# A Poisson loss on one Trainium2 core: one load instead of four ahead of the first barrier, the others after ScalarE's table load

## The chip, the core and the metric

The kernel runs on one core of a Trainium2 chip. The metric is the device time of an execution in microseconds, the median of several runs. A profile shows one execution as a *span*, from the first instruction counted to the last landing. Every ratio below is the mean time of one kernel's fast runs over that of the kernel before in the same rounds on the same chip, so it is not quite the ratio of the medians quoted beside it.

## The reference

```
log_input: [1024, 4096] float32      target: [1024, 4096] float32
loss = exp(log_input) - target * log_input
out  = mean(loss, axis=-1)           # 1024 values
```

The two inputs are 33.55 MB together and are read once. The result is 4 KB.

## The kernel before

Each of the 128 partitions holds eight rows of both inputs. ScalarE takes the exponential of `x` (the input `log_input`) with a running sum, VectorE multiplies `t` (`target`) by `x` with a running sum, and a small ScalarE activation joins the two sums of a row. SyncE issues all loads into one queue: four rows of `x`, four of `t`, two of each, one of each, and the last row in seven pieces (`TAIL`).

```
loads = []
for first, rows in ((0, 4), (4, 2), (6, 1)):
    loads += [("x", first * d, rows * d), ("t", first * d, rows * d)]
for what, w in TAIL:                         # the last row, in pieces
    loads.append((what, at[what], w * d // 128))
    ...
early = []
for i, (what, lo, w) in enumerate(loads):
    if what == "x" and lo in (6 * d, 7 * d): # buffers come free here
        nc.sync.wait_ge(exp_done, free)
        nc.sync.wait_ge(prod_done, free)
    dma = nc.sync.dma_start(out=place(what, lo, w), in_=src[:, lo : lo + w])
    dma.then_inc(landed[i] if i < len(loads) - 1 else last_ready, 16)
    if lo < 6 * d:
        early.append(dma.ins)                # x_big, t_big, x_mid, t_mid
before_first_barrier(nc, early)              # moved ahead of SyncE's first drain
...
    nc.scalar.activation(out=e_dump[...], in_=place("x", lo, w), func=ACT_F.Exp,
                         accum_out=...).wait_op(landed[i], 16, "sem-ge")
```

A program begins with a barrier of all engines. `before_first_barrier` moves the given loads in front of it, so that data flow while the engines meet. Four loads go there: `x_big` and `t_big` (8.39 MB each), `x_mid` and `t_mid` (4.19 MB each). ScalarE's function table is loaded by an instruction of its own right before the first exponential, behind the barrier.

Of the kernel before, what the change touches and what calls it, by code (L numbers as in the profile page):

```python
# [5 lines left out]
ACT_F = mybir.ActivationFunctionType  # L6
ALU = mybir.AluOpType
F32 = mybir.dt.float32
# [5 lines left out]
def before_first_barrier(nc, instructions):  # L14





    here, first = nc.cur_bb.bb, nc.main_func.blocks[0]  # L20
    names = {i.name for i in instructions}
    here.instructions = [i for i in here.instructions if i.name not in names]
    at = next(
        k
        for k, i in enumerate(first.instructions)
        if i.engine == mybir.EngineType.SP and i.opcode == "Drain"
    )
    first.instructions = first.instructions[:at] + instructions + first.instructions[at:]


def kernel(tc, log_input, target, out):
# [14 lines left out]
    nc = tc.nc  # L46
# [3 lines left out]
    P = nc.NUM_PARTITIONS  # L50
    n, d = log_input.shape
# [41 lines left out]
    def place(what, lo, w):  # L93
        row = lo // d
        if 4 <= row < 6:
            return mid[what][:, lo - 4 * d : lo - 4 * d + w]
        if row >= 6:
            lo -= (6 if row == 6 else 4) * d
        return big[what][:, lo : lo + w]
# [4 lines left out]
    join_dump = nc.alloc_sbuf_tensor("join_dump", [P, 2 * last_row], F32).ap()  # L104
# [5 lines left out]
    landed = [nc.alloc_semaphore(f"landed{i}") for i in range(len(loads) - 1)]  # L110


    last_ready = nc.alloc_semaphore("last_ready")
    exp_done = nc.alloc_semaphore("exp_done")
    prod_done = nc.alloc_semaphore("prod_done")
    join_done = nc.alloc_semaphore("join_done")
    ones_done = nc.alloc_semaphore("ones_done")
    loss_done = nc.alloc_semaphore("loss_done")
    out_done = nc.alloc_semaphore("out_done")


    early = []
    for i, (what, lo, w) in enumerate(loads):
        if what == "x" and lo in (6 * d, 7 * d):
            free = 1 if lo == 6 * d else 4
            nc.sync.wait_ge(exp_done, free)
            nc.sync.wait_ge(prod_done, free)  # L127
        src = x_v if what == "x" else t_v
        dma = nc.sync.dma_start(out=place(what, lo, w), in_=src[:, lo : lo + w])  # L129
        dma.then_inc(landed[i] if i < len(loads) - 1 else last_ready, 16)  # L130
        if lo < 6 * d:
            early.append(dma.ins)
    before_first_barrier(nc, early)


    nc.gpsimd.memset(big["x"][:, 4 * d : 4 * d + n_parts], -1.0).then_inc(ones_done, 1)  # L136


    def join(row, exps):
        nc.scalar.wait_ge(exp_done, exps)  # L140
        nc.scalar.activation(  # L141
            out=join_dump[:, 2 * row : 2 * row + 2],
            in_=parts[:, 2 * row : 2 * row + 2],
            func=ACT_F.Copy,
            scale=inv_d,
            accum_out=all_loss[:, row : row + 1],
        ).wait_op(prod_done, row + 1, "sem-ge").then_inc(join_done, 1)

    for k, (lo, w, i) in enumerate(x_work):
# [3 lines left out]
        elif col == 0 and row == 1:  # L153
            nc.scalar.wait_ge(exp_done, k)
        nc.scalar.activation(  # L155
            out=e_dump[:, col : col + w],
            in_=place("x", lo, w),
            func=ACT_F.Exp,
            bias=0.0,
            scale=1.0,  # L160
# [8 lines left out]
    for j, (lo, w, i) in enumerate(t_work):  # L169
# [4 lines left out]
        if j < n_t - 1:  # L174
            nc.vector.tensor_tensor_reduce(  # L175
                out=place("t", lo, w),
                in0=place("t", lo, w),
                in1=place("x", lo, w),
                scale=-1.0,
# [9 lines left out]
        else:  # L189
# [4 lines left out]
                out=place("t", lo, w + n_parts),  # L194
                in0=place("t", lo, w + n_parts),
                in1=place("x", lo, w + n_parts),
                scale=-inv_d,
# [8 lines left out]
    nc.sync.dma_start(out=out_v, in_=all_loss).wait_op(loss_done, 1, "sem-ge").then_inc(  # L206
        out_done, 16
    )
    used = landed + [last_ready, exp_done, prod_done, join_done, ones_done, loss_done]
    nc.sync.sem_clear(range(used[0].num, out_done.num))  # L210
    assert all(used[0].num <= s.num < out_done.num for s in used)
    nc.sync.wait_ge(out_done, 16).then_inc(out_done, -16)
# [30 lines left out]
```

## Time and profile before

| | before |
|---|---|
| device time, median of the first 3 runs | 84.07 us (84.0 to 84.13) |
| span of the profiled run | 82.5 us |
| DMA queue's packets, share of 16 engines | 95.8% |
| VectorE, ScalarE busy | 43%, 40% |
| the four early issues | 0.00 to 1.87 us |
| table load | 2.93 to 4.21 us |
| first exponential, first product | 21.80 us, 41.12 us |

The question to ask of such a table is which row sets the end. The longest waits of the two compute engines answer it (engine, line, what it waited for, us in total, times, the longest one):

```profile
DVE t_big L175 <- DMA t_big<-in_target_dram: 43.4, 3, 41.1
ACT e_dump L155 <- DMA x_big<-in_log_input_dram: 23.6, 3, 17.6
```

Both compute engines stand still until data come. The prediction below reads the rest of the profile.

### The profile page before, as it was taken

The page shows a single profiled execution, that of the slowest core. Times are in us where ns is not written, and L with a number is a line of the kernel's source. Part 1 is how long each engine was busy: PE and PEld are TensorE (multiplying, and loading weights), DVE is VectorE, ACT ScalarE, POOL GpSimd, SP SyncE. Part 2 cuts the span into 40 slices and gives each one's busy share as a digit, 9 for nine tenths or more (in the row PEclk, how much of TensorE's full clock was granted, in tenths as well). Part 3 has the DMA queues.
Part 4 walks back from the last instruction along what each step waited for, and adds up shares of the span by engine and source line. Part 5 has one row for each costly group of instructions (what it writes and reads, how often), then busy time and mean ns, then how long its engine had stood idle before and what let it go on. Part 6 is the DMA issues. An engine that isn't in the chain of part 4 may idle for free.

```text
span 82.5 us, 131 instructions
## 1 busy us (share of the span) xinstructions
DVE 35.6 (43%) x22; ACT 33.2 (40%) x35; POOL 0.3 (0%) x5
## 2 busy tenths in 40 slices
DVE  0000000000000000000099999999369995993992
ACT  0500000000499920000000998979792496009460
POOL 0000000000000000000000000000000000000000
DMA  9289999929999992999599799799799999999960
GB/s 508 127 381 508 508 508 508 476 95 445 508 508 508 508 413 95 508 508 508 254 508 429 333 508 492 318 460 508 302 453 397 461 421 418 426 402 412 397 231 2
DMA packets 2016, 33.56 MB, mean 407 GB/s; under 512 B 352, under 2 KB 608, under 8 KB 1120
## 3 DMA queue, kind: packets, MB, share of 16 engines
q1 hardware_dynamic: 2016, 33.56, 95.8%
HBM read 33.55 MB, written 0.00 MB: 407 GB/s over the span
## 4 chain that ended last, share of the span: by engine, by line
DMA 72%; DVE 18%; issue 5%; SPq 3%; DVEq 0%
DMA t_big<-in_target_dram 49%; DMA x_big<-in_log_input_dram 23%; DVE t_big L175 17%; SPq L129 3%; DVE t_big L193 1%; DVE parts L175 0%; DVEq L192 0%; SPq L127 0%; DVE all_loss L193 0%
## 5 line engine op out<-in xcount | busy, mean ns | idle before, releaser
L175 DVE CUSTOM_DVE_ANT_0 t_big<-t_big,x_big 128x4096 f32<-128x4096 f32 (+3 forms) x8 | 26.2, 3308 | 43.5 <-DMA t_big<-in_target_dram 43.4
L155 ACT ACTIVATE e_dump<-x_big 128x4096 f32<-128x4096 f32 (+3 forms) x8 | 21.8, 2729 | 23.9 <-DMA x_big<-in_log_input_dram 23.6
L141 ACT ACTIVATE join_dump<-parts 128x2 f32<-128x2 f32 x7 | 1.4, 203 | 20.4 <-DVE parts L175 20.3
L175 DVE CUSTOM_DVE_ANT_0 t_mid<-t_mid,x_mid 128x4096 f32<-128x4096 f32 x2 | 8.8, 4424 | 2.0 <-DMA t_mid<-in_target_dram 2.0
L155 ACT ACTIVATE e_dump<-x_mid 128x4096 f32<-128x4096 f32 x2 | 7.1, 3568 | 0.0
L155 ACT ACT_TABLE_LOAD x1 | 1.3, 1283 | 2.9 <-PEq L48 2.9
L155 ACT ACTIVATION_READ_ACCUMULATOR e_dump<-x_big 128x1 f32 x8 | 1.5, 186 | 0.0
L141 ACT ACTIVATION_READ_ACCUMULATOR join_dump<-parts 128x1 f32 x7 | 1.3, 186 | 0.0
L175 DVE DVE_READ_ACCUMULATOR2_ANT parts<- 128x1 f32 x7 | 0.6, 84 | 0.0
L193 DVE CUSTOM_DVE_ANT_0 t_big<-t_big,x_big 128x390 f32<-128x390 f32 x1 | 0.6, 566 | 0.0
L155 ACT ACTIVATION_READ_ACCUMULATOR e_dump<-x_mid 128x1 f32 x2 | 0.4, 186 | 0.0
L175 DVE DVE_READ_ACCUMULATOR2_ANT t_big<- 128x1 f32 x3 | 0.2, 82 | 0.0
L136 POOL MEMSET x_big<- 128x6 f32 x1 | 0.1, 104 | 2.5 <-POOLq L48 2.5
L227 POOL MEMSET const-uint8-127<- 128x1 uint8 x1 | 0.1, 102 | 0.0
L227 POOL MEMSET const-bfloat16-1.0<- 128x1 bf16 x1 | 0.1, 101 | 0.0
L227 POOL MEMSET const-float32-0.0<- 128x1 f32 x1 | 0.1, 98 | 0.2 <-issue 0.2
L227 POOL MEMSET const-float32-1.0<- 128x1 f32 x1 | 0.1, 98 | 0.0
L193 DVE DVE_READ_ACCUMULATOR2_ANT all_loss<- 128x1 f32 x1 | 0.1, 82 | 0.0
## 6 DMA issues: line engine op xcount, KB each, us to landing
x_mid<-in_log_input_dram SPq DMA_DIRECT2D x1, 4096.0 KB, 49.9
t_mid<-in_target_dram SPq DMA_DIRECT2D x1, 4096.0 KB, 59.2
x_big<-in_log_input_dram SPq DMA_DIRECT2D x1, 2048.0 KB, 19.8
t_big<-in_target_dram SPq DMA_DIRECT2D x1, 2048.0 KB, 24.3
x_big<-in_log_input_dram SPq DMA_DIRECT2D x1, 1568.0 KB, 15.4
t_big<-in_target_dram SPq DMA_DIRECT2D x1, 800.0 KB, 17.0
t_big<-in_target_dram SPq DMA_DIRECT2D x1, 768.0 KB, 18.4
x_big<-in_log_input_dram SPq DMA_DIRECT2D x1, 384.0 KB, 18.9
```

The source lines that it names most:

```text
L129: dma = nc.sync.dma_start(out=place(what, lo, w), in_=src[:, lo : lo + w])
L136: nc.gpsimd.memset(big["x"][:, 4 * d : 4 * d + n_parts], -1.0).then_inc(ones_done, 1)
L141: nc.scalar.activation(out=join_dump[:, 2 * row : 2 * row + 2], in_=parts[:, 2 * row : 2 * row + 2], func=ACT_F.Copy, scale=inv_d, accum_o ...
L155: nc.scalar.activation(out=e_dump[:, col : col + w], in_=place("x", lo, w), func=ACT_F.Exp, bias=0.0, scale=1.0, accum_out=parts[:, 2 * ro ...
L175: nc.vector.tensor_tensor_reduce(out=place("t", lo, w), in0=place("t", lo, w), in1=place("x", lo, w), scale=-1.0, scalar=0.0, op0=ALU.mult ...
L193: nc.vector.tensor_tensor_reduce(out=place("t", lo, w + n_parts), in0=place("t", lo, w + n_parts), in1=place("x", lo, w + n_parts), scale= ...
L227: nc = _bacc.Bacc("TRN2", target_bir_lowering=False, num_devices=1)
```

## The change

Its intent is to let the engines through the first barrier sooner and to have ScalarE's table ready at once. Only the first load stays ahead of the barrier. A dummy exponential of a constant makes ScalarE load its table right after the barrier, and SyncE waits for it before it issues the second load.

```diff
+    table_done = nc.alloc_semaphore("table_done")
...
-    early = []
     for i, (what, lo, w) in enumerate(loads):
...
-        if lo < 6 * d:
-            early.append(dma.ins)
-    before_first_barrier(nc, early)
+        if i == 0:
+            before_first_barrier(nc, [dma.ins])
+            nc.sync.wait_ge(table_done, 1)
...
+    nc.scalar.activation(
+        out=join_dump[:, :1],
+        in_=nc.const_aps.tensor(0.0, [P, 1], F32),
+        func=ACT_F.Exp,
+        bias=0.0,
+        scale=1.0,
+    ).then_inc(table_done, 1)
```

The list of semaphores cleared at the end gets `table_done` too.

More of the change, by code (lines that the diff above doesn't have):

```diff
@@ L208 @@
     )
-    used = landed + [last_ready, exp_done, prod_done, join_done, ones_done, loss_done]
+    used = landed + [last_ready, exp_done, prod_done, join_done, ones_done, table_done, loss_done]
     nc.sync.sem_clear(range(used[0].num, out_done.num))
```

## The prediction

> **What bounds the kernel now.** I read the page first: the engine shares, the strip of 40 slices, and the chain that ended last.
>
> ```profile
> DVE 35.6 (43%) x22; ACT 33.2 (40%) x35; POOL 0.3 (0%) x5
> DMA  9289999929999992999599799799799999999960
> q1 hardware_dynamic: 2016, 33.56, 95.8%
> DMA 72%; DVE 18%; issue 5%; SPq 3%; DVEq 0%
> ```
>
> No compute engine is busy for half of the 82.5 us span, while the packets of the single queue fill 95.8% of the time of all 16 DMA engines. The few low digits in the DMA strip look like holes, so I asked for busy time in long stretches (columns after the window's length: DVE, ACT and POOL busy with instruction counts, PE clock, DMA share, GB/s).
>
> ```profile
> 1.00:21.00 20.00, 0.00 (x0) 1.28 (x1) 0.10 (x1) 1.00 1.02 426
> 21.00:41.00 20.00, 0.00 (x0) 7.42 (x4) 0.00 (x0) 1.00 1.01 439
> 41.00:61.00 20.00, 17.93 (x9) 14.06 (x15) 0.00 (x0) 1.00 0.98 424
> 61.00:80.00 19.00, 16.66 (x11) 9.99 (x15) 0.00 (x0) 1.00 0.99 410
> ```
>
> The share is about 1 from 1 us to 80 us: there are no holes. A packet is counted in the slice in which it starts, and packets of 2.4 us beat against slices of 2.06 us. So the loads are one unbroken stream.
>
> The DMA issues give the same stream by landings.
>
> ```profile
> x_mid<-in_log_input_dram SPq DMA_DIRECT2D x1, 4096.0 KB, 49.9
> t_mid<-in_target_dram SPq DMA_DIRECT2D x1, 4096.0 KB, 59.2
> x_big<-in_log_input_dram SPq DMA_DIRECT2D x1, 21.8
> t_big<-in_target_dram SPq DMA_DIRECT2D x1, 40.7
> ```
>
> These are us from issue to landing. With the issue times of the timeline (0.00, 0.43, 0.89, 1.37 us) the first four loads land at 21.8 (x_big, 8.39 MB), 41.1 (t_big, 8.39 MB), 50.8 (x_mid, 4.19 MB) and 60.6 us (t_mid, 4.19 MB). The steps are 19.3, 9.7 and 9.8 us, or 8.39 MB / 19.3 us = 435 GB/s each time. All of 33.55 MB at that rate take 77.1 us. Add 21.8 - 19.3 = 2.5 us, the start-up and landing latency of the first load, and the data would be in at 79.6 us. The chain of waits has its last load landing at 61.04 + 18.91 = 79.95 us, 0.35 us later, which I put down to the small tail loads. From there to the end of the span are 2.6 us: the last pieces of VectorE to 81.07 us, the store issued at 81.10 and landing 1.4 us after. The timed 84.07 us hold another 1.5 us outside the span, which no part of the diff names.
>
> So the time is start-up 2.5 + stream 77.5 + end 2.6 + outside 1.5 = 84.1 us. Only what delays the first byte, breaks the stream, or lengthens the end can move it.
>
> **What the Trainium skill says.**
> 1. "ScalarE: Activation LUTs", section "What ACT_TABLE_LOAD costs": a table load takes about 1283 ns whatever the set, and the page adds a drain of about 1380 ns for a switch. The trace agrees on the load, a single one of 1283 ns. It doesn't show the drain: ScalarE's drains around the barrier last 8 ns.
> 2. "DMA: Bandwidth & Descriptors", section "Anatomy of one DMA": a DMA engine does not wait on semaphores; the wait is on the issuing sequencer. So the added wait holds SyncE, not the load already in flight. The trace before has the same form: the load of 45.64 us waited for both compute engines on SyncE while the DMA share stayed 0.98.
> 3. Same page, "Queues, rings and completion order": each DMA engine takes the descriptors of one queue in ring order. The landings above agree: each load lands one transfer time after the one ahead of it. A load issued early into the same ring therefore only stands in line.
> 4. Same page, "Where 436 GB/s comes from": a ceiling of 435.2 GB/s. The 435 GB/s from the landings are at it, so a different order of issue has no rate to win.
>
> **The change, part by part.** The lines of the start, before (the timeline, start and duration in us):
>
> ```profile
> 0.00 0.38 SPq L129 DMA_DIRECT2D x_big<-in_log_input_dram  x1
> 0.43 0.42 SPq L129 DMA_DIRECT2D t_big<-in_target_dram  x1
> 0.89 0.43 SPq L129 DMA_DIRECT2D x_mid<-in_log_input_dram  x1
> 1.37 0.50 SPq L129 DMA_DIRECT2D t_mid<-in_target_dram  x1
> 2.93 1.28 ACT L155 ACT_TABLE_LOAD   x1 [2.93 <-PEq L48]
> 21.80 3.59 ACT L155 ACTIVATE e_dump<-x_big 128x4096 f32<-128x4096 f32 x1 [17.58 <-DMA x_big<-in_log_input_dram]
> ```
>
> *Kept:* x_big is still the first SyncE instruction, ahead of the barrier, so the stream should begin at the same 1 us. The built program confirms it: on SyncE only the branch moves up, between the first load and the other three.
>
> *Moved:* three issues leave the front of the barrier. SyncE reaches it at 0.38 instead of 1.87 us, 1.49 us earlier; GpSimd's constants end at 0.43 us and hold it no longer. In the trace before, the table load began 2.93 - 1.87 = 1.06 us after the last early issue. I keep this distance: the table load then starts near 1.45 us and ends near 2.73 us.
>
> *Added:* one exponential of 128x1. The 128x2 activations of the joins take 203 ns, so it ends near 2.95 us. It writes a scratch tile that the joins overwrite later on the same engine. The wait on SyncE then lets t_big go near 3.0 us instead of 0.43; x_mid and t_mid follow near 3.5 and 3.9, done near 4.4 us. No second table load appears in the built program: it moves from the first real exponential to the dummy one.
>
> *What lies on the path:* t_big's descriptors are needed when the first DMA engine has finished its part of x_big. x_big lands at 21.8 us; taking off the whole start-up of 2.5 us as a generous landing latency leaves 19.3 us. Against 3.5 us for the end of its issue that is a reserve of some 16 us. The delay of 2.6 us costs nothing. On the other side, the table load ending 1.5 us sooner wins nothing either, as the last line above shows: ScalarE waits 17.58 us for x_big after its table load.
>
> *The end:* clearing one more semaphore is part of a single range clear that covers the row of semaphores anyway. I count 0.
>
> Sum: 84.07 + 0 (delayed issue hidden) + 0 (earlier table hidden) + 0 (dummy exponential in idle time), about 84.05 us.
>
> **The rivals.**
> *A, the new wait opens a hole.* The stream would stop if t_big came after x_big's packets ran out. For it: the wait chains SyncE to ScalarE, which it was free of. Against it: 16 us of reserve, and the trace before shows a much tighter case without harm. The load of x_big at 58.69 us was issued 1.9 us before t_mid, the last load then queued, landed at 60.6 us, and the stretches on both sides show a share of 0.98 and 0.99. A hole of 1 us would make 85.1 us; over 2% needs 1.7 us, an issue at about 21 us.
>
> *B, the earlier barrier is worth its 1.5 us.* If something of the start were on the path behind the barrier, the time would be 84.07 - 1.5 = 82.6 us, still within 2%. Against it: after the barrier every engine waits for data, VectorE for 41.1 us and ScalarE for 17.6 us, and the data do not wait for the barrier.
>
> *C, the early issues disturb the first load.* Windows of half a microsecond show the first packets to be slow.
>
> ```profile
> 1.00:1.50 0.50, 0.00 (x0) 0.00 (x0) 0.00 (x0) 1.00 5.89 1966
> 4.00:4.50 0.50, 0.00 (x0) 0.21 (x1) 0.00 (x0) 1.00 4.54 1966
> ```
>
> Both windows hold starts worth 1966 GB/s x 0.5 us = 983 KB, 15 packets of 64 KB. A share of 5.89 x 16 engines x 0.5 us / 15 = 3.14 us per packet, against 2.42 us in the next round. The first round runs while SyncE issues the other three. If the extra 0.7 us came from that and not from filling an empty pipe, the change would give part of it back: 83.4 us at best. Against it: six issues crowd into 59 to 62 us and the share there stays full, so issues do not slow a running stream visibly. I take the 0.7 us for the latency of a first read, which stays. Or the disturbance moves to the second round with the issues, again a zero.
>
> **Range and chances.** The three runs before span 0.13 us. The main line gives no change; C allows a gain of up to 0.7 us, with a small chance, B less, A next to nothing. So 84.05 us, eighty per cent range 83.75 to 84.25. Faster by over 2% means under 82.39 us, more than B and its whole 1.5 us could give: 0.01. Slower by over 2% means over 85.75 us, a hole of 1.7 us: 0.01. Within 2%: 0.98.
>
> **What would show it.** Right: t_big issued near 3.0 us but landing still at 41.1 us, so its time to landing falls from 40.7 to about 38; table load near 1.45 us and ScalarE's wait for x_big longer by the same 1.5 us; full DMA share in the four long stretches; last load landing at 79.95 us. Wrong: x_big landing before 21.5 us (C); a share well under 1 around 21 us or t_big landing after 41.3 us (A); a wait of SyncE at the end that is shorter or longer than 1.4 us of store; or a difference between the timed run and the span that is not 1.5 us, something the trace does not show and I would have missed.

## The result and the profile after

The changed kernel takes 84.05 us (median of 6 runs, 83.91 to 84.4), the kernel before 84.02 us in the same rounds (83.98 to 84.13). The ratio is 1.0006 with a 95% interval of 0.9987 to 1.0025: the same.

The timeline of the start of the changed kernel (start, duration, engine, instruction; in brackets the idle time before and its releaser):

```profile
1.44 1.28 ACT L140 ACT_TABLE_LOAD   x1 [1.44 <-PEq L48]
2.73 0.20 ACT L140 ACTIVATE join_dump<-const-float32-0.0 128x1 f32<-128x1 f32 x1
2.96 0.33 SPq L129 DMA_DIRECT2D t_big<-in_target_dram  x1
3.34 0.43 SPq L129 DMA_DIRECT2D x_mid<-in_log_input_dram  x1
3.82 0.44 SPq L129 DMA_DIRECT2D t_mid<-in_target_dram  x1
21.96 3.59 ACT L164 ACTIVATE e_dump<-x_big 128x4096 f32<-128x4096 f32 x1 [19.03 <-DMA x_big<-in_log_input_dram]
```

The start did change. The table is loaded 1.49 us sooner (1.44 instead of 2.93 us), and `t_big` is issued 2.53 us later (2.96 instead of 0.43 us). But ScalarE's wait for `x_big` grew from 17.58 to 19.03 us, so the time won at the barrier is spent waiting for the same load.

The long stretches of the changed kernel (length, busy time of DVE, ACT and POOL with counts, clock, DMA share, GB/s):

```profile
1.00:21.00 20.00, 0.00 (x0) 1.49 (x2) 0.10 (x1) 1.00 0.99 416
21.00:41.00 20.00, 0.00 (x0) 7.42 (x4) 0.00 (x0) 1.00 1.03 446
41.00:61.00 20.00, 17.73 (x9) 13.88 (x15) 0.00 (x0) 1.00 0.98 422
61.00:80.00 19.00, 16.65 (x11) 10.08 (x14) 0.00 (x0) 1.00 0.99 411
```

The stream is as unbroken as before. The first two rows differ by 0.03 and 0.02 from before, as a packet counts in the stretch where it starts; their sums agree to 0.01 (0.99 + 1.03 against 1.02 + 1.01).

The issues (KB of one where given, us from issue to landing) say how the delay vanished:

```profile
x_big<-in_log_input_dram SPq DMA_DIRECT2D x1, 21.9
t_big<-in_target_dram SPq DMA_DIRECT2D x1, 38.3
```

`t_big` took 40.7 us from issue to landing before and takes 38.3 us now. It was issued 2.5 us later and stood in line 2.4 us less. It lands at 2.96 + 38.3 = 41.3 us, against 41.1 us.

The chain that ended last must be read with care here. Its head in the changed kernel (start, duration, what):

```profile
1.44 1.28 ACT L140
2.72 0.01 issue
2.73 0.21 ACT join_dump L140
2.94 0.02 issue
2.96 38.33 DMA t_big<-in_target_dram
41.28 0.02 issue
```

Read naively, it says that the table load and the dummy exponential begin the path that sets the end, so that 1.5 us of it could be saved. They do release the issue of `t_big`, but the 38.33 us that follow are not the length of that transfer. They include the time in which it stood in line behind `x_big`. The chain goes from a load back to its issue, not to the load ahead of it in the queue. The experiments show which of the two it is.

### The profile page after: what moved, and what is told of

Same layout as the page of the kernel before. It is cut to its first block, busy times and chain, and to the rows that moved or that the text cites. A ratio compares the mean times of both kernels' runs of the same rounds, so it can differ in the third digit from the quotient of the medians.

```text
span 82.8 us, 132 instructions
## 1 busy us (share of the span) xinstructions
DVE 35.6 (43%) x22; ACT 33.4 (40%) x36; POOL 0.3 (0%) x5
## 4 chain that ended last, share of the span: by engine, by line
DMA 69%; DVE 20%; issue 6%; ACT 2%; SPq 1%; DVEq 0%
DMA t_big<-in_target_dram 69%; DVE t_big L184 19%; ACT L140 2%; SPq L129 1%; DVE t_big L202 1%; ACT join_dump L140 0%; DVE parts L184 0%; DVEq L201 0%; SPq L127 0%; DVE all_loss L202 0%
## 5 line engine op out<-in xcount | busy, mean ns | idle before, releaser
L164 ACT ACTIVATE e_dump<-x_big 128x4096 f32<-128x4096 f32 (+3 forms) x8 | 21.8, 2730 | 25.3 <-DMA x_big<-in_log_input_dram 25.0
L140 ACT ACT_TABLE_LOAD x1 | 1.3, 1283 | 1.4 <-PEq L48 1.4
## 6 DMA issues: line engine op xcount, KB each, us to landing
t_big<-in_target_dram SPq DMA_DIRECT2D x1, 2048.0 KB, 24.3
x_big<-in_log_input_dram SPq DMA_DIRECT2D x1, 384.0 KB, 18.9
```

What stands on the lines that cost most here:

```text
L140: nc.scalar.activation(out=join_dump[:, :1], in_=nc.const_aps.tensor(0.0, [P, 1], F32), func=ACT_F.Exp, bias=0.0, scale=1.0,).then_inc(tab ...
L164: nc.scalar.activation(out=e_dump[:, col : col + w], in_=place("x", lo, w), func=ACT_F.Exp, bias=0.0, scale=1.0, accum_out=parts[:, 2 * ro ...
```

## The experiments

Theory: the time is the start-up of the first load, then one stream at the DMA engines' rate, then the work after the last landing. An issue that comes before the queue runs dry is free, whatever it waits for. The rivals: (A) the later issue costs something, (B) the earlier barrier wins something, (C) issuing three loads at once slows the first packets. An A and a B of the same size would also give a zero, so each was tested by itself.

### How late may the second load be: 17, 21 and 24 us

Three kernels delay `t_big` further. Instead of the 128x1 exponential, ScalarE does n = 4, 5 or 6 exponentials of a constant, 4096 wide, and SyncE waits for the last.

```diff
-            nc.sync.wait_ge(table_done, 1)
+            nc.sync.wait_ge(table_done, n)
...
-    nc.scalar.activation(out=join_dump[:, :1], in_=<constant 128x1>, ...)
+    for k in range(n):
+        if k:
+            nc.scalar.wait_ge(table_done, k)
+        nc.scalar.activation(out=e_dump[:, :d], in_=<constant 128x4096>, ...
+            ).then_inc(table_done, 1)
+    nc.scalar.wait_ge(table_done, n)
```

The waits between the exponentials are there because all of them write the same tile: without the waits, the check before the chip turns the program down for a race.

Expected with four:

> As the changed kernel, but the second load waits for four wide exponentials of a constant (128x4096, some 3.6 us each) after the table load: t_big goes near 2.7 + 4 x 3.7 = 17.5 us. Hidden-issue theory: if the queue were empty, t_big would land 21.8 us after its issue (the latency of the first load of the kernel before), and it lands at 41.1 us when it stands in line, so an issue up to 41.1 - 21.8 = 19.3 us is free: 84.0 us, within 0.3 us of before, with 14 us more work on ScalarE. Rival (the queue needs the second load much sooner than that, for example while its descriptors are being laid down): slower by 1 us or more.

Expected with five:

> Five wide exponentials: t_big goes near 2.7 + 5 x 3.7 = 21.2 us. Hidden-issue theory: 21.2 - 19.3 = 1.9 us past the free reserve, so 84.0 + 1.9 = 85.9 us, with t_big landing near 43.0 us. Rival: no edge at all here, as compute is what bounds, and it has slack: 84.0 us.

Expected with six:

> Six wide exponentials: t_big goes near 2.7 + 6 x 3.7 = 24.9 us. Hidden-issue theory: 24.9 - 19.3 = 5.6 us past the reserve, 89.6 us; against the run with five the time grows by one exponential, 3.7 us, one for one. Rival (the engines catch up on part of a hole): less than 3 us more than with five.

| n | `t_big` issued | issue to landing | this (median) | before, same rounds | ratio (95%) |
|---|---|---|---|---|---|
| 4 | 17.18 us | 23.9 us | 84.23 us | 84.14 us | 1.0007 (0.9976 to 1.0037) |
| 5 | 20.82 us | 21.8 us | 85.80 us | 84.14 us | 1.019 (1.0158 to 1.0222) |
| 6 | 24.42 us | 21.8 us | 89.17 us | 84.14 us | 1.0589 (1.056 to 1.0618) |

With four, `t_big` goes 14 us later than in the changed kernel, ScalarE does over 14 us more work, and the time stays the same. With five and six the time to landing stops at 21.8 us, which is that of a load into an empty queue, like `x_big` at the very start. The issue and the time to landing stand in the chains of the three kernels (start, us, what), for four, five and six:

```profile
17.18 23.92 DMA t_big<-in_target_dram
20.82 21.80 DMA t_big<-in_target_dram
24.42 21.77 DMA t_big<-in_target_dram
```

From there every microsecond counts: from five to six the issue moves by 3.60 us and the time by 3.37 us. The median span of the same runs grows by the whole 3.6 us, from 84.1 to 87.7 us: with five, 1.7 us of the device time lie outside the span, with six 1.5 us. No view says why. The edge follows from each alone: 20.82 - (85.80 - 84.14) = 19.2 us, and 24.42 - (89.17 - 84.14) = 19.4 us. With spans (82.8 us before) both give 19.5 us. The landings had put it at 41.1 - 21.8 = 19.3 us. The hole itself can be seen with six, first the issue of `t_big`, then the windows of that kernel:

```profile
24.42 0.33 SPq L129 DMA_DIRECT2D t_big<-in_target_dram  x1
...
21.00:25.30 4.30, 0.00 (x0) 4.20 (x2) 0.00 (x0) 1.00 0.00 0
25.20:26.20 1.00, 0.00 (x0) 1.00 (x1) 0.00 (x0) 1.00 3.13 1049
```

No packet starts between 21.0 and 25.3 us; then all 16 engines start within the microsecond, 1049 GB/s x 1 us = 16 packets of 64 KB. This rules out A at 2.96 us, with 16 us to spare, as far as the interval of the run with four reaches (0.3 us), and it rules out a bound by compute.

### The first packets without issues beside them

The run with four answers C too: for 17 us nothing is issued behind the first load. The window in which the first packets start, in the kernel before:

```profile
0.90:1.90 1.00, 0.00 (x0) 0.00 (x0) 0.00 (x0) 1.00 3.12 1049
```

and with four exponentials:

```profile
0.90:1.90 1.00, 0.00 (x0) 0.48 (x1) 0.10 (x1) 1.00 3.20 1049
```

Both hold 16 packets, so the share times 16 engines times 1 us over 16 packets is the mean packet: 3.12 us beside three other issues, 3.20 us beside none. The first round at 25.2 us of the run with six, shown above, gives 3.13 us. Each figure is from one profile. The issues do not slow the first packets. The 0.7 us over the 2.42 us of later rounds are there both times a load meets an empty queue, at 1 us and at 25 us alike.

### The same wait ahead of the first load

```diff
     for i, (what, lo, w) in enumerate(loads):
+        if i == 0:
+            nc.sync.wait_ge(table_done, 1)
...
-        if i == 0:
-            before_first_barrier(nc, [dma.ins])
-            nc.sync.wait_ge(table_done, 1)
```

> The same wait for the table put ahead of the first load, which then goes behind the barrier like all others. Theory: the first load is on the path with every nanosecond, so the whole 2.96 us at which t_big was issued in the changed kernel is added: 84.0 + 2.96 = 87.0 us. Rival (the launch or the barrier hides the start of the stream too): under 85 us.

It took 86.99 us against 84.14 us, ratio 1.0327 (1.03 to 1.0354). The load that before went at 0.00 now reads:

```profile
2.91 0.38 SPq L131 DMA_DIRECT2D x_big<-in_log_input_dram  x1
```

The time grew by 2.85 us for 2.91 us of delay. Two things delay the load here: it goes behind the barrier, which alone makes its issue 1.38 us late (next experiment), and it waits for the table, the other 1.53 us. Both are paid: the time is 2.85 us longer here and 1.37 us longer without the wait. So the wait that costs nothing ahead of the second load costs its whole length ahead of the first.

### No load ahead of the barrier

```diff
-        if i == 0:
-            before_first_barrier(nc, [dma.ins])
-            nc.sync.wait_ge(table_done, 1)
```

> No load ahead of the barrier, no wait for the table (the dummy exponential stays). Theory: x_big goes when the barrier lets the engines go, 1.44 us in the changed kernel, so 84.0 + 1.4 = 85.4 us. Rival (the barrier is reached sooner when SyncE issues nothing ahead of it): 84.4 to 85.0 us.

It took 85.46 us against 84.09 us, ratio 1.0164 (1.015 to 1.0179), a loss of 1.37 us. The load went here:

```profile
1.38 0.36 SPq L129 DMA_DIRECT2D x_big<-in_log_input_dram  x1
```

So moving one load ahead of the barrier is worth 1.37 us, and the first load alone earns all of it.

### The two parts of the change, one at a time

First the changed kernel without SyncE's wait for the table; `t_big` goes at 1.42 us.

```diff
-            nc.sync.wait_ge(table_done, 1)
```

> The changed kernel without the wait for the table: one load ahead of the barrier, the second near 1.5 us. Theory: 84.0 us, as both, since any issue before 19 us is free. Rival (the table wait costs something that a gain of the earlier barrier makes up for): faster than the changed kernel by 0.2 us or more.

It took 84.11 us against 84.09 us, ratio 1.0003 (0.9992 to 1.0015). Then the kernel before plus the dummy exponential alone, with four loads ahead of the barrier:

```diff
+    nc.scalar.activation(out=join_dump[:, :1], in_=<constant 128x1>, ...
+        ).then_inc(table_done, 1)
```

> The kernel before plus the dummy exponential alone: all four loads ahead of the barrier. Theory: 84.0 us, the exponential runs in the 17.6 us in which ScalarE waits for x_big. Rival (the exponential or the table load costs something by itself): slower than the kernel before by 0.2 us or more.

It took 84.01 us against 84.09 us, ratio 0.9996 (0.9982 to 1.001). Each part by itself is worth nothing beyond the intervals (0.15 us either way), so the zero is not a loss and a gain that cancel. The first of the two is also the test of B. Its ScalarE passes the barrier at 1.43 us instead of 2.93 us, no wait takes the gain back, and still the time is the same:

```profile
1.43 1.28 ACT L139 ACT_TABLE_LOAD   x1 [1.43 <-PEq L48]
```

### The changed kernel once more

No edit; more rounds, run together with the three runs before this one, as the first profile had `x_big` 0.16 us later than before.

> The changed kernel once more, in five rounds, on the chip of these runs, to bound the difference: theory 84.0 us, ratio between 0.998 and 1.002. Rival (a small real loss, as the first profile has x_big landing 0.16 us later): 84.15 to 84.3 us, ratio over 1.0015 with the interval above 1.

It took 84.05 us against 84.09 us, ratio 1.0004 (0.9987 to 1.0021). In this profile `x_big` lands at 21.7 us and the span is 82.5 us, as in the kernel before. The 0.16 us lie within the scatter of profiles: the first exponential on `x_big` starts at 21.80 and 21.86 us in two profiles with four loads ahead of the barrier, and at 21.73, 21.96 and 22.05 us in three with one.

### A cut at the end instead of the start

If the start has nothing to give, the end might. The tail of the last row was cut differently, on the kernel before and on the changed one:

```diff
-TAIL = [("x", 98), ("t", 50), ("t", 48), ("x", 24), ("t", 18), ("x", 6), ("t", 12)]
+TAIL = [("x", 98), ("t", 24), ("t", 36), ("t", 38), ("x", 24), ("t", 18), ("x", 6), ("t", 12)]
```

> The kernel before with its tail of small loads cut otherwise: the two pieces of t of 50 and 48 become 24, 36 and 38 (units of 32 columns; the rest unchanged). In the kernel before VectorE is idle for 1.28 us before the piece of 50 lands and is then behind to the end: its last piece begins 0.55 us after the last load has landed. With a first piece of 24 it starts 0.98 us sooner at the price of one more fixed start of some 0.2 us; the last load lands when it did. Stream theory (only the start, the stream and the work after it count): some 0.3 us less, 83.7 us, ratio near 0.997. Rival (the end is set by the last landing alone, or one more small load costs as much as is won): 84.0 us.

> The changed kernel with the same cut of the tail. Stream theory: the change at the start adds nothing to this either, so 83.7 us, equal to the run on the kernel before within 0.15 us. Rival (start and tail interact): it differs by 0.3 us or more.

Both missed: 84.13 us and 84.12 us against 84.07 us, ratios 1.0011 (0.9997 to 1.0026) and 1.0007 (0.9993 to 1.0022). The two agree with each other, so the start and the tail do not interact, but the 0.3 us did not come. The kernel before, piece of 576 columns of `t`, its two last issues of `t` (KB, us to landing) and the last product:

```profile
79.70 0.76 DVE L175 CUSTOM_DVE_ANT_0 t_big<-t_big,x_big 128x576 f32<-128x576 f32 x1
80.50 0.57 DVE L193 CUSTOM_DVE_ANT_0 t_big<-t_big,x_big 128x390 f32<-128x390 f32 x1
...
t_big<-in_target_dram SPq DMA_DIRECT2D x1, 288.0 KB, 19.2
t_big<-in_target_dram SPq DMA_DIRECT2D x1, 192.0 KB, 18.9
```

The new tail on the kernel before, same pieces:

```profile
79.88 0.76 DVE L175 CUSTOM_DVE_ANT_0 t_big<-t_big,x_big 128x576 f32<-128x576 f32 x1 [0.32 <-DMA t_big<-in_target_dram]
```

VectorE did get ahead: it now idles 0.32 us for the piece of 576 columns. But that piece lands at 79.9 us and no sooner. In the kernel before it was issued at 60.52 us and landed 19.2 us later, at 79.7 us, just as VectorE came free; there was no backlog to win. The last load was to land when it did before; it lands near 80.6 us (62.00 + 18.6) instead of 80.4, about as much later as the whole profiled run was longer (84.07 against 83.89 us). SyncE needed 1.67 us to issue that load, the eighth piece, and 1.71 us on the changed kernel, against 0.46 us for the last piece before; no view says why. The load then still stood in line for over 16 us, so this is not on the path. In the kernel before, the last piece of `t`, issued at 61.52 us, landed 18.9 us later, at 80.4 us, and the last product starts at 80.50 us. I had taken 79.95 us for the last landing, the one the chain of waits goes through, which is that of the small piece of `x` ahead of it. One reserve remains: the last piece's semaphore is also raised by the two compute engines, so that this one landing is less certain than the others. No version here beats the kernel before.

## Why the prediction was right

*The stream as the bound.* It forecast 84.05 us and got 84.05 us. That the two agree to the hundredth is luck: the median of the kernel before alone moved between 84.02 and 84.14 us from one set of rounds to another. That the four terms add up to 84.1 us shows nothing either, as all were read from the time before. The experiments test them: 2.91 us before the first byte gave 2.85 us, and a second load 5.1 us past the edge (24.42 - 19.3) gave 5.03 us.

*The times of the change.* Table load at 1.45 us: measured 1.44. Dummy exponential done near 2.95 us: 2.73 + 0.21 = 2.94. `t_big` issued near 3.0 us: 2.96. Time to landing near 38 us: 38.3.

*The reserve.* The prediction took 19.3 us as the latest useful issue on a deliberately cautious guess, the whole start-up counted as landing latency. Measured, the edge is at 19.2 to 19.5 us. So the guess, called generous, was by luck the true figure: a load that meets an empty queue pays that whole start-up again.

*Rival A* is ruled out by the run at 17.18 us, *rival B* by the run without the wait, *rival C* by the first packets at 3.20 us with no issue beside them.

*One argument against A was misread.* The prediction calls the load of 58.69 us a "much tighter case", issued 1.9 us before the landing of `t_mid`, "the last load then queued". It was not the last: the two loads of the seventh row, issued at 45.64 and 46.02 us, stood behind it and landed at 65.4 and 70.3 us (46.02 + 24.3). The lead was 11.6 us, and the trace before shows no tight case. Only the runs with 17 to 24 us show how close an issue may come.

*Two terms were mis-sized.* The 1.5 us outside the span are the difference of two executions, the median time of the timed runs and the span of the profiled one, which itself took 83.89 us. Within one execution it is 1.3 to 1.4 us, 1.3 us in the changed kernel (84.09 - 82.8), so the sign that named 1.5 us would have misled. And of the 0.35 us put down to the small tail loads, some 0.2 us were lost earlier: `x_mid` and `t_mid` took 9.7 + 9.8 = 19.5 us, not 19.3.

*One more step was off without touching the sum.* The end was told as the last load landing at 79.95 us and 1.1 us of VectorE after it. By the issue view the last load lands near 80.4 us, and the product after it starts within 0.1 us. The total from the stream's start to the end is the same, but the split was wrong, and the tail experiment that rested on it missed. One of its own signs was also set too finely: it named a landing of `t_big` after 41.3 us as a mark of A. The profiled run had 41.28 us, and the run without the wait 41.35 us, at no loss of time. Both had `x_big` landing later too, which is scatter.

## What to carry to other kernels

When transfers stand in one queue that never runs dry, as here, only the issue of the first one is on the path. Put that one ahead of everything; whether the next went one or fifteen microseconds later did not matter, as long as it arrived before the line ended. The latest free issue could be read from the profile: the landing time of the load in line minus the issue-to-landing time of a load of the same size into an empty queue. And a chain of waits that runs through an issue with a long transfer behind it names a suspect, not a cost, since the transfer's time includes its time in line.

## What the Trainium skill lacked or had wrong

- "ScalarE: Activation LUTs", "What ACT_TABLE_LOAD costs": the load of 1283 ns is exact here, but the drain of about 1380 ns added for a switch is not seen on the first load. In the changed kernel the load runs from 1.44 to 2.72 us and the exponential starts at 2.73 us. No run here switches between two sets.
- "DMA: Bandwidth & Descriptors", "Latency and other measured facts": about 600 ns to the first byte for this kind of issue, without saying from where it is counted. Here no packet starts before 25.3 us for an issue that runs from 24.42 to 24.75 us: it is at least 0.55 us from the end of the issue and nearly 0.9 us from its start. The first round of packets then takes 3.1 us instead of 2.42 us.
- The same page, "Anatomy of one DMA", gives a fixed cost of about 2.0 us, measured for transfers issued from GpSimd. For a load of 8.39 MB issued from SyncE into an empty queue the runs show 21.8 us, 2.5 us over the 19.3 us that it takes in line.
- No page says what a load ahead of the program's first barrier is worth (1.37 us here), nor how late a load behind it may be issued at no cost (19.2 to 19.5 us here).
